# Moving q tiles, the v tile and a z tile to earlier projection stages in a hybrid layer

## The chip, the core and the metric

The kernel runs on one core of a Trainium2 chip. The metric is device time in microseconds (us) of one execution. A core has TensorE (PE; PEld is its weight load), VectorE (DVE), ScalarE (ACT), GpSimd (POOL) and SyncE (SP, which only issues DMAs here). Each works through its own queue in order, and they wait for each other by semaphores.

## The reference

One decoder layer on 1024 tokens of width 1024. One input projection feeds two mixers: a state space scan (Mamba-2, 16 heads in 2 groups, chunks of 128 tokens), and attention over the 256 best keys per query, which a small indexer scores. Their outputs are concatenated and projected, then comes a gated feed-forward network with a convolution.

```python
proj = x @ w_in                                     # 1024 x 4696
z, xbc, dt_raw, q, k, v, qi, ki, wi = split(proj)
xbc = silu(causal_dwconv(xbc, width 4))             # x: 1024, B: 256, C: 256 columns
y = ssd_scan(xs, dt, a, bm, cm) + d_skip * xs       # 8 chunks, state carried on
y_ssd = rms_norm(y * silu(z), by group) * ssd_norm_g
score = sum_h wi[h] * relu(qi[h] @ ki.T)            # causal
keep = top 256 of score per query
y_att = softmax(q @ k.T / 8 on keep) @ v
m = concat(y_ssd, y_att) @ w_out
h = layer_norm(alpha * x + m)
out = layer_norm(alpha * h + (silu(gate) * up) @ w_down)   # gate, up = dwconv(h @ w_up, width 3)
```

## The kernel before

All matmuls of the projections are made of three: weights and inputs are split into a high and a low part, and `three` (L157 to L161) adds high by high, high by low and low by high. A weight tile is loaded by SyncE (L140, L151), its high part made by GpSimd (L129) and its low part too (L132).

The input projection is cut into tiles. Tiles "c" 0 to 11 are the convolution's columns (8 and 9 are B of the two groups, 10 and 11 are C, 0 to 3 and 4 to 7 the x columns of the two groups), "q" 0 to 7 and "k" 0 and 1 the attention's columns, of 128 columns each; "z" 0 to 3 and "v" 0 are tiles of 256 columns. A c, q or k tile is two halves of 24 matmuls, 128x512 each (`proj` in PSUM). A z or v tile is eight blocks of 24 matmuls, 128x256 each (`tps`). ScalarE evicts each of them. q, k, v and z are stored to DRAM and loaded again later; a c tile stays on chip: ScalarE makes the first tap of the convolution (L481), VectorE the three others (L484), ScalarE the SiLU, and for x columns TensorE transposes it (`xsp`) into `xs`.

Beside the projections run, as generators that yield after each step:

- the scores (L303 to L309), while stage 0 of the projections runs;
- the search for the 256th best score (`topk_gen`): 32 rounds, one bit each. In a round three blocks of queries are counted on VectorE (L347) and three on ScalarE (L350), then VectorE makes the next candidate (L355, L357, L364). Behind the rounds come the masks of six blocks, L384 to L407, all on VectorE;
- the state space scan of each group (`ssd_gen`), 8 chunks: a DMA (L522), ScalarE (L526, L528), VectorE (L532, L533), GpSimd (L536 to L540), TensorE (`yoff`, `stps`, `yps`), VectorE (`off` L547, `state` L555, `xs` L563);
- the gate of each group (`gate_gen`), which loads z again (L572) and ends with transposes (`yT`) that are stored for the output projection;
- the load of k (`k_load`).

A table, `STAGES`, has the order of the projection tiles: stage 0 beside the scores, stage 1 alone, stage 2 beside the scan of group 0, stage 3 beside the gate of group 0, and stage 4 beside `k_load`, the scan of group 1 and then its gate. `par` takes a step of each in turn, and `weave` takes two steps of the search for every five of all this. The order of SyncE's queue is the order in which the code is written. On the other engines a scheduler orders the instructions when the kernel is built, by priority (the scan's is raised by 100) and by its own estimate of when each is ready; from then on the order is fixed. Behind all this come the q and v loads and the attention, whose first matmuls are `lgps` (L677).

Of the kernel before, what the change touches and what calls it, by code (L numbers as in the profile page):

```python
# [57 lines left out]
def hybrid_layer(ctx, tc, x, w_in, ssd_conv_w, ssd_conv_b, dt_bias, a_log, d_skip, ssd_norm_g,  # L58
# [18 lines left out]
    def big(name, dtype=F32, shape=(P, 1024), tag="t4"):  # L77
        return pool.tile(list(shape), dtype, name=name, tag=tag, bufs=BUFS[tag])

    def bank(name, tag, shape=(P, 512)):  # L80
        return psum.tile(list(shape), F32, name=name, tag=tag, bufs=PBUFS[tag])
# [236 lines left out]
    def topk_gen():  # L318
# [56 lines left out]
        for e, ch in enumerate(CHAINS):  # L375
            for i, (b, eng) in enumerate(ch):
# [32 lines left out]


    STAGES = ([("k", 0), ("k", 1), ("q", 0), ("q", 1), ("q", 2), ("c", 8), ("c", 10)],
# [4 lines left out]
    stream = [("c", QI0 + t * P) for t in range(1, 4)]  # L416
    for kind, i in [u for st in STAGES for u in st]:
        if kind in "ckq":
# [20 lines left out]
    for t in range(4):  # L439
        w = w_qi if t == 0 else next_w()  # L440
        a, c = big("qsa", F32R, tag="pp"), big("qsb", F32R, tag="pp")
# [594 lines left out]
    for j in range(NF):  # L1036
# [13 lines left out]
        c = bank("pc", "tp")  # L1050
# [221 lines left out]
```

## Time and profile before

| | us |
|---|---|
| median of 3 runs | 1705.73 (1703.85 to 1708.65) |
| profiled execution | 1701.0 |
| its span, first to last instruction | 1699.1 |
| PE busy | 1590.0 (94%) |
| DVE busy | 1218.1 (72%) |
| ACT busy | 917.5 (54%) |
| POOL busy | 882.0 (52%) |

A busy share is a mean over the whole span, and the stages differ. The slices of the profile show PE at nine tenths or more in most of them, and at seven to eight tenths in some between 200 and 510 us, where the search runs and DVE is at nine. Matmuls overlap, so the time of one in a row (0.39 us) is longer than the distance to the next. An "idle before" in brackets is time in which the engine had nothing to run, and the name behind the arrow is what ended it.

### The profile page before, as it was taken

Reading aid. Unit: us, or ns where it says so; the run is one execution under the profiler, and the core shown is the slowest. Engines: PE = TensorE matmul, PEld = TensorE weight load, DVE = VectorE, ACT = ScalarE, POOL = GpSimd, SP = SyncE. Lnnn points to the kernel's source line nnn. Section 1 sums busy time; section 2 is a strip of 40 time slices with the busy share of each in tenths; the row PEclk is TensorE's granted clock in tenths of the full one; section 3 lists DMA queues with packets and bytes.
Section 4 is the critical chain, followed back from the end, with each engine's and each line's share of the span. In section 5 each row is a group of like instructions: output and inputs, shape, how many; then the busy total and the mean of one; then the engine's idle time right before and its main releaser. Section 6 shows DMA issues by size and latency. Waiting matters only on the chain.

```text
span 1699.1 us, 23245 instructions
## 1 busy us (share of the span) xinstructions
PE 1590.0 (94%) x7844; PEld 1319.0 (78%) x7844; DVE 1218.1 (72%) x2274; ACT 917.5 (54%) x1759; POOL 882.0 (52%) x659
## 2 busy tenths in 40 slices
PE   8999998797989989999999993999999999999997
PEld 6888887685878867777888772878888888878886
DVE  2644689999893467777787479677777777756468
ACT  3433597687633566676676444555555555542141
POOL 2153225644257253555464356666777676475490
PEclk9999998998989999999999995999999999999999
DMA  5042032131433664554454442233444433698782
GB/s 172 16 123 63 17 103 84 43 109 57 131 91 99 179 193 110 149 151 131 147 153 151 157 162 74 87 118 131 140 138 136 132 118 118 225 351 299 237 278 109
DMA packets 208846, 232.86 MB, mean 137 GB/s; under 512 B 14051, under 2 KB 138327, under 8 KB 208727
## 3 DMA queue, kind: packets, MB, share of 16 engines
q1 hardware_dynamic: 160999, 159.79, 31.4%
q10 hardware_dynamic: 47728, 71.58, 11.6%
q8 instruction: 62, 1.02, 0.3%
q14 instruction: 57, 0.47, 0.1%
HBM read 159.70 MB, written 71.63 MB: 136 GB/s over the span
## 4 chain that ended last, share of the span: by engine, by line
PE 47%; DVE 5%; DMA 2%; ACT 1%; issue 1%; POOL 0%; SPq 0%; ACTq 0%; DVEq 0%; POOLq 0%
PE acc L159 4%; PE acc L160 4%; PE acc L161 4%; PE pa L159 2%; PE pd L159 2%; PE pa L161 2%; PE pa L160 2%; PE pc L159 2%; PE pc L160 2%; PE pd L161 2%; PE pc L161 2%; PE pd L160 2%; PE ops L160 2%; PE ops L159 2%; PE ops L161 2%; PE ptp L692 2%
## 5 line engine op out<-in xcount | busy, mean ns | idle before, releaser
L159 PE MATMUL proj<-xTh,w_hi 128*128 128x512 f32 (+1 forms) x432 | 173.0, 401 | 7.0 <-ACT xbc L478 3.5
L161 PE MATMUL proj<-xTh,w_lo 128*128 128x512 f32 (+1 forms) x432 | 170.7, 397 | 2.9 <-POOL w_lo L132 2.9
L160 PE MATMUL proj<-xTl,w_hi 128*128 128x512 f32 (+1 forms) x432 | 171.5, 397 | 0.0
L686 POOL TENSOR_SCALAR prob<-prob,sm 128x512 f32<-128x512 f32 (+7 forms) x128 | 97.1, 769 | 142.8 <-DVE sm L685 104.6
L999 POOL TENSOR_TENSOR w_hl<-s,w_hl 128x512 fp32r<-128x512 f32 x88 | 121.4, 1385 | 61.3 <-ACT w_hl L998 57.0
L129 POOL TENSOR_SCALAR w_hi<-w_raw 128x1024 fp32r<-128x1024 f32 x35 | 46.3, 1325 | 184.4 <-PE proj L160 124.4
L132 POOL TENSOR_TENSOR w_lo<-w_raw,w_hi 128x1024 fp32r<-128x1024 f32 (+1 forms) x45 | 113.1, 2516 | 27.1 <-ACT w_hi L131 24.9
L160 PE MATMUL acc<-wd_hl,g_hl 128*128 128x512 f32 x308 | 120.4, 391 | 0.0
L161 PE MATMUL acc<-wd_hl,g_hl 128*128 128x512 f32 x308 | 120.1, 391 | 0.0
L999 POOL TENSOR_TENSOR w_hl<-w_raw,w_hl 128x512 fp32r<-128x512 f32 x66 | 90.3, 1371 | 55.9 <-ACT w_hl L998 53.7
L683 ACT ACTIVATE prob<-prob,mx 128x512 f32<-128x512 f32 (+7 forms) x128 | 98.5, 771 | 36.6 <-DVE mx L680 35.9
L694 ACT ACTIVATE pt<-ptp 128x512 fp32r<-128x512 f32 x144 | 81.3, 595 | 64.7 <-PE ptp L692 43.7
L159 PE MATMUL acc<-wd_hl,g_hl 128*128 128x512 f32 x308 | 112.5, 392 | 3.3 <-ACT wd_hl L1157 3.3
L159 PE MATMUL ops<-w_hi,y_hi 128*128 128x512 f32 x256 | 102.4, 400 | 6.1 <-ACT y_hi L131 3.2
L350 ACT ACTIVATE junk<-score,cand 128x1024 bf16<-128x1024 f32 (+2 forms) x96 | 86.0, 895 | 38.5 <-DVE cand L364 35.4
L695 DVE TENSOR_TENSOR pt<-ptp,pt 128x512 fp32r<-128x512 f32 x144 | 95.6, 685 | 15.1 <-ACT pt L694 14.6
L1158 POOL TENSOR_TENSOR wd_hl<-keep,wd_hl 128x512 fp32r<-128x512 f32 x55 | 81.4, 1505 | 44.8 <-ACT wd_hl L1157 42.1
L159 PE MATMUL tps<-w_hi,xTh 128*128 128x256 f32 x320 | 95.8, 300 | 8.8 <-ACT tout L614 7.6
L159 PEld LDWEIGHTS proj<-xTh,w_hi 128*128 128x128 f32 (+1 forms) x432 | 82.2, 190 | 26.2 <-ACT xbc L478 3.9
L160 PE MATMUL ops<-w_lo,y_hi 128*128 128x512 f32 x256 | 101.5, 396 | 0.4 <-DVE w_lo L132 0.4
L161 PE MATMUL ops<-w_hi,y_lo 128*128 128x512 f32 x256 | 100.4, 395 | 0.0
L161 PEld LDWEIGHTS proj<-xTh,w_lo 128*128 128x128 f32 (+1 forms) x432 | 81.8, 189 | 21.0 <-POOL w_lo L132 4.1
(346 smaller groups left out, 5010.1 us busy)
## 6 DMA issues: line engine op xcount, KB each, us to landing
w_raw<-in_ffn_w_up_dram SPq DMA_DIRECT2D x44, 512.0 KB, 4.0
g_hl<-gs_dr SPq DMA_DIRECT2D x44, 512.0 KB, 5.5
w_raw<-in_w_in_dram SPq DMA_DIRECT2D x36, 512.0 KB, 4.9
r_dr<-rout ACTq DMA_DIRECT2D x48, 256.0 KB, 2.2
g_dr<-gt ACTq DMA_DIRECT2D x33, 256.0 KB, 2.9
keep<-in_ffn_w_down_dram SPq DMA_DIRECT2D x33, 256.0 KB, 5.7
acsb<-a_dr SPq DMA_DIRECT2D x16, 512.0 KB, 4.2
w_raw<-in_w_out_dram SPq DMA_DIRECT2D x16, 512.0 KB, 4.4
```

What stands on the lines that cost most here:

```text
L129: nc.gpsimd.tensor_scalar(hi, raw, 1.0, 1.0, op0=OP.mult, op1=OP.mult)
L132: (nc.vector if lo_on_dve else nc.gpsimd).tensor_tensor(lo, raw, f(hi), op=OP.subtract)
L159: nc.tensor.matmul(ps, ah, bh, start=start, stop=False, skip_group_check=onto)
L160: nc.tensor.matmul(ps, ah, bl, start=False, stop=False, skip_group_check=onto)
L161: nc.tensor.matmul(ps, al, bh, start=False, stop=stop, skip_group_check=onto)
L350: nc.scalar.activation(junk[1][:, :n], score_ap[b], AF.Sign, bias=c, scale=-1.0, accum_out=val[e][:, i:i + 1])
L683: nc.scalar.activation(t[:, :w], t[:, :w], AF.Exp, bias=mx[:, h:h + 1], scale=-1.0, accum_out=sm[:, h:h + 1])
L686: nc.gpsimd.tensor_scalar(t[:, :w], t[:, :w], sm[:, 4 + h:5 + h], 1.0, op0=OP.mult, op1=OP.mult)
L694: nc.scalar.activation(pt[:, 0], ps, AF.Copy)
L695: nc.vector.tensor_tensor(pt[:, 1], ps, f(pt[:, 0]), op=OP.subtract)
L999: nc.gpsimd.tensor_tensor(t[:, 1], src, f(t[:, 0]), op=OP.subtract)
L1158: nc.gpsimd.tensor_tensor(wt[:, 1], w_raw, f(wt[:, 0]), op=OP.subtract)
```

## The change

Only the table differs. Tiles q 3 and q 4 move from stage 2 to stage 1, between the c tiles; q 5 and v 0 move from stage 4 to stage 2; z 2 moves from stage 4 to stage 3, between c 4 and c 5. Stage 4 keeps z 3, q 6 and q 7.

```diff
     STAGES = ([("k", 0), ("k", 1), ("q", 0), ("q", 1), ("q", 2), ("c", 8), ("c", 10)],
-              [("c", 0), ("c", 1), ("c", 2), ("c", 3)],
-              [("z", 0), ("z", 1), ("q", 3), ("q", 4)],
-              [("c", 9), ("c", 11), ("c", 4), ("c", 5), ("c", 6), ("c", 7)],
-              [("z", 2), ("z", 3), ("v", 0), ("q", 5), ("q", 6), ("q", 7)])
+              [("c", 0), ("q", 3), ("c", 1), ("c", 2), ("q", 4), ("c", 3)],
+              [("z", 0), ("z", 1), ("q", 5), ("v", 0)],
+              [("c", 9), ("c", 11), ("c", 4), ("z", 2), ("c", 5), ("c", 6), ("c", 7)],
+              [("z", 3), ("q", 6), ("q", 7)])
```

VectorE's queue before, at the end of the search and the start of the masks. `cand` is the search's candidate, `conv_3559` is c 5, `conv_3670` is c 6, and L384 is the first operation of the masks:

```order
L364 SCALAR_TENSOR_TENSOR cand0_4340<-fail0_4338,cand0_4324 128x2
L484 SCALAR_TENSOR_TENSOR conv_3559<-xbc_3560,cw_656,conv_3559 128x1023
L357 TENSOR_TENSOR fail1_4346<-val1_1579,thr1_1578 128x4
L484 SCALAR_TENSOR_TENSOR conv_3559<-xbc_3560,cw_656,conv_3559 128x1022
L364 SCALAR_TENSOR_TENSOR cand1_4348<-fail1_4346,cand1_4334 128x4
L484 SCALAR_TENSOR_TENSOR conv_3559<-xbc_3560,cw_656,conv_3559 128x1021
L484 SCALAR_TENSOR_TENSOR conv_3670<-xbc_3671,cw_656,conv_3670 128x1023
L484 SCALAR_TENSOR_TENSOR conv_3670<-xbc_3671,cw_656,conv_3670 128x1022
L484 SCALAR_TENSOR_TENSOR conv_3670<-xbc_3671,cw_656,conv_3670 128x1021
L384 TENSOR_SCALAR eq_4510,cnt_4511<-score_693,cand0_4340 128x1024
```

The same place after the change; `conv_3731` is c 4, `conv_4197` is c 5, `conv_4312` is c 6. Ahead of these rows, behind the last candidate, stand the taps of c 9, the eight L585 of group 0's gate and the taps of c 11:

```order
L484 SCALAR_TENSOR_TENSOR conv_3731<-xbc_3732,cw_656,conv_3731 128x1023
L484 SCALAR_TENSOR_TENSOR conv_3731<-xbc_3732,cw_656,conv_3731 128x1022
L484 SCALAR_TENSOR_TENSOR conv_3731<-xbc_3732,cw_656,conv_3731 128x1021
L484 SCALAR_TENSOR_TENSOR conv_4197<-xbc_4198,cw_656,conv_4197 128x1023
L484 SCALAR_TENSOR_TENSOR conv_4197<-xbc_4198,cw_656,conv_4197 128x1022
L484 SCALAR_TENSOR_TENSOR conv_4197<-xbc_4198,cw_656,conv_4197 128x1021
L484 SCALAR_TENSOR_TENSOR conv_4312<-xbc_4313,cw_656,conv_4312 128x1023
L484 SCALAR_TENSOR_TENSOR conv_4312<-xbc_4313,cw_656,conv_4312 128x1022
L384 TENSOR_SCALAR eq_4784,cnt_4785<-score_693,cand0_4614 128x1024
L387 TENSOR_SCALAR pen_4787<-score_693,cand0_4614 128x1024
L484 SCALAR_TENSOR_TENSOR conv_4312<-xbc_4313,cw_656,conv_4312 128x1021
```

The masks stand behind c 6 in both; the taps of the other c tiles have moved from between the rounds to behind them, while z 2 has moved to between c 4 and c 5 in TensorE's queue.

TensorE's queue before, at the seventh chunk of group 1 (`yoff`, `stps` and `yps` belong to the scan, `tps` to the v tile):

```order
L160 MATMUL tps_4908<-w_lo_4748,xTh_113 128x256
L545 MATMUL yoff_5054<-state_4867,conv_3272 128x512
L161 MATMUL tps_4908<-w_hi_4747,xTl_121 128x256
L159 MATMUL tps_4908<-w_hi_4747,xTh_113 128x256
L160 MATMUL tps_4908<-w_lo_4748,xTh_113 128x256
L161 MATMUL tps_4908<-w_hi_4747,xTl_121 128x256
L159 MATMUL tps_4991<-w_hi_4555,xTh_114 128x256
```

The fifth to the seventh chunk of group 1 after the change, from the last projection on (`ops` is the output projection):

```order
L161 MATMUL proj_5106<-xTh_117,w_lo_4933 128x512
L545 MATMUL yoff_5183<-state_5093,conv_3606 128x512
L551 MATMUL stps_5188<-xdd_5178,btok_5158 128x512
L561 MATMUL yps_5193<-xdt_5177,lmat_5162 128x64 x8
L545 MATMUL yoff_5243<-state_5190,conv_3606 128x512
L551 MATMUL stps_5248<-xdd_5231,btok_5158 128x512
L561 MATMUL yps_5253<-xdt_5230,lmat_5215 128x64 x8
L545 MATMUL yoff_5300<-state_5250,conv_3606 128x512
L551 MATMUL stps_5305<-xdd_5288,btok_5158 128x512
L561 MATMUL yps_5310<-xdt_5287,lmat_5272 128x64 x8
```

The last four chunks have no projection between them any more; one chunk more and then `ops` and `yT` follow.

## Rows read from the trace of the kernel before

**Rows 1.** The page's head.

```profile
span 1699.1 us, 23245 instructions
```

**Rows 2.** Windows: length; busy PE, PEld, DVE, ACT, POOL; clock; DMA share, GB/s.

```profile
353.00:429.00 76.00, 66.44 (x279) 52.80 (x278) 69.59 (x153) 60.73 (x122) 31.63 (x19) 0.91 0.27 82
429.00:505.00 76.00, 66.79 (x453) 60.39 (x452) 74.30 (x106) 39.35 (x89) 29.30 (x19) 0.93 0.40 117
505.00:556.00 51.00, 48.55 (x350) 43.72 (x350) 22.69 (x28) 17.82 (x42) 36.22 (x28) 0.97 0.35 98
556.00:600.00 44.00, 44.00 (x219) 37.12 (x219) 18.43 (x21) 23.73 (x45) 14.14 (x7) 1.00 0.67 193
```

**Rows 3.** Timeline of VectorE, end of the search: start, length, instruction, idle before.

```profile
423.77 0.16 DVE L364 SCALAR_TENSOR_TENSOR cand<-fail,cand 128x4 int32<-128x4 int32 x1
423.89 1.28 DVE L484 SCALAR_TENSOR_TENSOR conv<-xbc,cw,conv 128x1021 f32<-128x1021 f32 x1
429.96 5.16 DVE L484 SCALAR_TENSOR_TENSOR conv<-xbc,cw,conv 128x1023 f32<-128x1023 f32 x3 [4.79 <-ACT conv L481]
435.04 1.27 DVE L384 TENSOR_SCALAR_CACHE_REDUCE eq<-score,cand 128x1024 bf16<-128x1024 f32 x1
```

**Rows 4.** Timeline of ScalarE, the eviction of c 6.

```profile
428.05 0.60 ACT L478 ACTIVATE xbc<-proj 128x512 f32<-128x512 f32 x1 [0.69 <-PE proj L161]
```

**Rows 5.** Timeline of VectorE, from the last mask to the last chunk.

```profile
503.87 1.57 DVE L407 SCALAR_TENSOR_TENSOR mask<-score,cand,eq 128x512 bf16<-128x512 f32 x1
...
533.15 0.69 DVE L547 TENSOR_TENSOR off<-yoff,dtset 128x512 f32<-128x512 f32 x1 [3.42 <-PE stps L551]
537.58 0.69 DVE L563 TENSOR_TENSOR xs<-yps,skip 128x512 f32<-128x512 f32 x1 [3.73 <-POOL skip L548]
...
545.63 0.69 DVE L547 TENSOR_TENSOR off<-yoff,dtset 128x512 f32<-128x512 f32 x1 [6.37 <-PE stps L551]
...
551.87 0.69 DVE L547 TENSOR_TENSOR off<-yoff,dtset 128x512 f32<-128x512 f32 x1 [3.17 <-PE yoff L545]
...
554.96 0.69 DVE L563 TENSOR_TENSOR xs<-yps,skip 128x512 f32<-128x512 f32 x1 [0.43 <-PE yps L561]
```

**Rows 6.** Timeline of TensorE, the attention's first matmul.

```profile
600.15 0.36 PE L677 MATMUL lgps<-kh,qst 128*128 128x256 f32 x1
```

**Rows 7.** Timeline of VectorE, rounds of the search with little between them.

```profile
353.40 1.13 DVE L347 TENSOR_SCALAR_CACHE_REDUCE junk<-score,cand 128x896 bf16<-128x896 f32 x1
...
361.51 1.15 DVE L347 TENSOR_SCALAR_CACHE_REDUCE junk<-score,cand 128x896 bf16<-128x896 f32 x1
```

**Rows 8.** Timeline of TensorE, the eighth chunk of group 0.

```profile
349.51 1.89 PE L561 MATMUL yps<-xdt,lmat 128*128 128x64 f32 x16
```

**Rows 9.** Timeline of TensorE: matmuls six apart (proj) and nine apart (tps).

```profile
456.83 0.28 PE L160 MATMUL tps<-w_lo,xTh 128*128 128x256 f32 x1
...
457.91 0.28 PE L160 MATMUL tps<-w_lo,xTh 128*128 128x256 f32 x1
...
592.76 0.39 PE L161 MATMUL proj<-xTh,w_lo 128*128 128x512 f32 x1
...
594.12 0.39 PE L161 MATMUL proj<-xTh,w_lo 128*128 128x512 f32 x1
```

**Rows 10.** Timeline of TensorE, its waits between 385 and 397 us.

```profile
389.39 0.50 PE L159 MATMUL proj<-xTh,w_hi 128*128 128x512 f32 x1 [1.87 <-POOL w_hi L129]
...
393.60 0.79 PE L159 MATMUL proj<-xTh,w_hi 128*128 128x512 f32 x1 [3.47 <-ACT xbc L478]
...
396.78 0.79 PE L161 MATMUL proj<-xTh,w_lo 128*128 128x512 f32 x1 [1.97 <-POOL w_lo L132]
```

**Rows 11.** Timeline of GpSimd, ahead of the wait at 537 us.

```profile
533.92 2.37 POOL L132 TENSOR_TENSOR w_lo<-w_raw,w_hi 128x1024 fp32r<-128x1024 f32 x1
```

**Rows 12.** Timeline of TensorE, the first chunk of group 1.

```profile
474.74 3.68 PE L561 MATMUL yps<-xdt,lmat 128*128 128x64 f32 x16 [2.49 <-DVE lmat L533]
```

## The prediction

> **What bounds the kernel now.** The profiled execution took 1701.0 us for a span of 1699.1 us [rows 1]. The runs have a median of 1705.73 us, 4.7 us above it. The sum below is made in the profiled execution, and its difference is added to the median.
>
> I first read the table by stretches. Between 353 and 600 us, where the change acts, TensorE is not the bound everywhere [rows 2]. Up to 505 us VectorE is busy for 69.59 of 76 and then 74.30 of 76 us, while TensorE has gaps and a granted clock of 0.91 and 0.93. From 505 us it turns round: VectorE works 22.69 of 51 us, and from 556 to 600 us TensorE is busy for all 44.00 us, with projections that nothing else waits for. So the stretch up to 505 us is paced by VectorE's queue, and the one behind it is filled by TensorE.
>
> Next, VectorE's own timeline at the seam [rows 3]. The bit search (L347 to L364) ends with its last `cand` at 423.77 us. From then on the masks of the attention could be made, beginning with L384. But L384 runs only at 435.04 us: ahead of it in VectorE's queue stand the taps (L484) of conv tiles 5 and 6, and tile 6's first tap waited 4.79 us for ScalarE's copy of the projection. This is the mechanism of my forecast, already there in small: the masks wait for TensorE's projection of conv tile 6. Its last matmul is done when ScalarE picks it up at 428.05 us [rows 4], 7.0 us ahead of L384.
>
> Then the way to the attention [rows 5, 6]: the last mask ends at 505.44 us, the last chunk of state space group 1 (its `xs`) starts at 554.96 us, and the first logits of the attention run at 600.15 us. The attention cannot start without the masks, and its q loads stand in SyncE's queue behind the gate of group 1.
>
> **The change part by part.** No instruction is added or removed; every tile still has its weight load on SyncE, its split on GpSimd and its stores on ScalarE's queue. What counts is where they stand. The order shows 5 steps.
>
> 1. The eighth chunk of group 0 comes later. TensorE's queue has more projections ahead of the first chunk, so VectorE goes further with the search before it: ahead of the eighth chunk's `xs` it has 76 passes of L347 where it had 63, and 9 conv taps where it had 6. Three passes make a round, and two rounds took 361.51 - 353.40 = 8.11 us where little else ran [rows 7]. So 13/3 x 4.06 = 17.6 us, and three taps of 1.28 us [rows 3] give 3.8 us, less 1 us as the search starts a little earlier: +20.4 us. The yps matmuls of that chunk ended at 349.51 + 1.89 = 351.4 us [rows 8] and now at 371.8 us. VectorE is nearly full here, so it cannot hide this; if it does, the term is 0.
>
> 2. From there to conv tile 6, TensorE has more to do. Before: 253 proj matmuls and 24 transposes. After: 236 proj, 323 tps (v and z tile 2) and 40 transposes. A proj takes (594.12 - 592.76)/6 = 0.227 us, a tps (457.91 - 456.83)/9 = 0.12 us [rows 9], and I count a transpose as a tps. That is 60.3 us before and 97.2 us after. Before, 351.4 to 428.05 is 76.7 us, so 16.4 us were lost, 7.3 us of them in three waits for weights and for an eviction that stood in ScalarE's queue among the search [rows 10]. After, only 20 of the search's 96 passes are left here (27 us of about 100), so I take 5 us lost; bounds 0 and 16.4. Tile 6 is projected at 371.8 + 97.2 + 5 = 474.0 us, 46 us later than before. The idle TensorE time that the moved work fills is real, but it lies where VectorE is waited for, and the fill stands ahead of what VectorE waits for next.
>
> 3. VectorE runs dry. The end of its search moves earlier (it has fewer taps of tiles 9, 11, 4 and 5 between its rounds), and then come the taps of tiles 11, 4, 5 and 6, with the masks behind them as before. What is queued behind the waiting tap is the whole mask block, and for that waits the attention. L384 moves from 435.04 to about 481 us. The block up to the last mask took 505.44 - 435.04 = 70.4 us and gets one more tap, so the last mask ends at 481 + 70.4 + 1.3 = 552.7 us, 47.3 us later.
>
> 4. The tail gets shorter. From the last mask to the first logits it took 600.15 - 505.44 = 94.7 us. Six chunks are left in it, before and after. Now the last four stand in TensorE's queue without projections between them, so VectorE's three long waits for TensorE (3.42, 6.37, 3.17 us) go, and so does the wait of 3.73 us for GpSimd [rows 5], which was splitting weights of a moved tile at 533.92 us [rows 11]: -16.7 us. Bounds: 0, if another link of the chunk chain is late next (GpSimd's five passes per chunk would be), and -28.3 us, all of VectorE's idle time in 505 to 556 [rows 2]. The gate, its loads of z and then of q keep their 45.2 us behind the last `xs`. First logits at 552.7 + 78.0 = 630.7 us, +30.6 us.
>
> 5. Behind the first logits the order is the same but for 8 transposes, about 1 us less. TensorE's projections no longer cover the tail: of its work between tile 6 and the first logits about 75 us are left of 132, and 474 + 75 = 549 us is well before 630, so TensorE is no bound there.
>
> Sum: +20.4 + 25.5 (97.2 + 5 - 76.7) + 1.3 - 16.7 - 1 = +29.5 us, rounded to +30: 1731 us for the profiled execution, 1736 us for the median. With the bounds of steps 2 and 4 alone it lies between +13 and +58.
>
> **The clock.** After a wait of 2.49 us the yps of one chunk took 3.68 us at a granted clock of one half, against 1.89 us [rows 8, 12], so 1.8 us more. In the tail after the change TensorE will wait before nearly every chunk. The Trainium skill (TensorE: Matmul & The Clock Gate, HAM oscillation) says that a kernel whose short bursts of matmuls are separated by waits falls back to the slow clock at each burst. By that rule the four bare chunks cost 4 x 1.8 = 7 us more, and the sum is +37; by the rows, where the chunks with full TensorE ran at 1.89 us, it is +30. I leave it in the upper part of the range.
>
> **Rivals.**
>
> A, faster: the eighth chunk is not late. If ScalarE's passes pace the search and VectorE does the additional rounds in time it now spends blocked, step 1 is 0. Tile 6 is then there at 454 us, 38 us of TensorE work later the first chunk of group 1 runs (492 us), and eight chunks at (49.5 - 13)/6 = 6.1 us and the gate's 45.2 us give 586 us, if the masks fit between the chunks: about -15 us, 1691 us. It decides once the masks no longer stand in front. For it: the chunk chain needs no mask. Against it: both are in one VectorE queue, whose order puts the last mask ahead of the third chunk, and VectorE was full.
>
> B, hardly a difference: step 1 as forecast, but the masks fit between the chunks. 474 + 38 + 49 + 45 = 606 us, +5 us, 1711 us. For it: VectorE has waits in the chunk chain to fill. Against it as in A.
>
> C, slower than forecast: 16 us lost in step 2 (z tile 2's weights are loaded behind the gate's z loads on SyncE), no gain in the tail, and the slow clock: 30 + 11 + 17 + 7 = +65 us, 1771 us; with one or two of the three, +40 to +55. For it: losses of this kind are in the trace. Against it: the waits of VectorE for TensorE lose their cause.
>
> **How the numbers follow.** Forecast 57% (its own range 1719 to 1746), A 12%, B 13%, C 18%. What a measurement can tell here is about 0.3%, 5 us. Faster by more than that: A, 12%. Within it: most of B, 9%. Slower: the rest, 79%. The range leaves a tenth on each side: below, the larger part of A (under 1700), above, the upper half of C (over 1757).
>
> **What would show it.** Right: the last `cand` well before 424 us, then L484 waiting for ScalarE's L481 for some 40 us in all before L384 near 481 us; the last mask near 553 us; in the last chunks TensorE waiting for VectorE and not the other way; first logits near 630 us. Wrong: L384 before 450 us, or the first logits before 600 us. If L384 is late and the logits are not, the mask block was not what the attention waited for, and step 3 fails. If the eighth chunk's `xs` is near 353 us, step 1 fails.

## The result, and the profile after

| | before | after |
|---|---|---|
| median | 1704.79 us (4 runs, 1703.65 to 1708.65) | 1725.47 us (4 runs, 1724.94 to 1728.46) |
| ratio, 95% interval | | 1.0123 [1.0111, 1.0136] |
| span of the profiled execution | 1699.1 us | 1723.4 us |
| first logits of the attention | 600.15 us | 625.54 us |
| from there to the end | 1098.9 us | 1097.8 us |

The change made the kernel slower by 20.7 us; 1736 were forecast, in a range of 1700 to 1757. The profiled executions differ by 24.3 us, all of it ahead of the first logits (+25.4 us there, -1.1 us behind them).

The head of the page answers to [rows 1]:

```profile
span 1723.4 us, 23264 instructions
```

The windows of the changed kernel answer to [rows 2], with one window more:

```profile
353.00:429.00 76.00, 68.85 (x381) 59.66 (x381) 67.98 (x162) 58.18 (x121) 33.98 (x22) 0.93 0.31 98
429.00:505.00 76.00, 75.93 (x506) 69.83 (x505) 29.19 (x34) 35.52 (x72) 23.47 (x12) 1.00 0.30 96
505.00:556.00 51.00, 44.12 (x248) 36.96 (x246) 50.65 (x82) 20.06 (x44) 19.84 (x14) 0.93 0.27 76
556.00:600.00 44.00, 26.63 (x116) 17.02 (x114) 22.37 (x28) 15.62 (x33) 31.11 (x25) 0.80 0.26 77
600.00:640.00 40.00, 19.71 (x80) 14.21 (x80) 23.56 (x52) 24.97 (x49) 9.51 (x8) 0.70 0.75 216
```

Between 429 and 505 us the two engines have changed places. TensorE is busy for 75.93 of 76 us where it was for 66.79, and VectorE for 29.19 where it was for 74.30. VectorE's work has slid into the next window (50.65 us for 22.69), and TensorE's idle time has gone to the end.

The seam on VectorE, which answers to [rows 3], in two pieces of its timeline (start, length, instruction, idle before):

```profile
408.63 0.16 DVE L364 SCALAR_TENSOR_TENSOR cand<-fail,cand 128x4 int32<-128x4 int32 x1
408.97 4.84 DVE L484 SCALAR_TENSOR_TENSOR conv<-xbc,cw,conv 128x1023 f32<-128x1023 f32 x3 [0.18 <-ACT conv L481]
...
432.39 4.74 DVE L484 SCALAR_TENSOR_TENSOR conv<-xbc,cw,conv 128x1023 f32<-128x1023 f32 x3 [5.43 <-ACT conv L481]
476.52 4.58 DVE L484 SCALAR_TENSOR_TENSOR conv<-xbc,cw,conv 128x1023 f32<-128x1023 f32 x3 [39.40 <-ACT conv L481]
484.70 2.60 DVE L484 SCALAR_TENSOR_TENSOR conv<-xbc,cw,conv 128x1023 f32<-128x1023 f32 x2 [3.60 <-ACT conv L481]
487.22 1.27 DVE L384 TENSOR_SCALAR_CACHE_REDUCE eq<-score,cand 128x1024 bf16<-128x1024 f32 x1
```

The search ends 15.1 us earlier than before, and the masks (L384) begin 52.2 us later. In one wait VectorE stands still for 39.40 us: its first tap of c 5 waits for ScalarE's tap (L481), that one for ScalarE's copies of the projection (L478), and those for TensorE, which works on z 2 first. ScalarE's timeline shows it (it answers to [rows 4]); of the copies, the first is the second half of c 4, the next two are c 5, the last two c 6:

```profile
430.05 0.60 ACT L478 ACTIVATE xbc<-proj 128x512 f32<-128x512 f32 x1 [2.00 <-PE proj L161]
...
462.01 0.60 ACT L478 ACTIVATE xbc<-proj 128x512 f32<-128x512 f32 x1 [5.08 <-PE proj L161]
...
469.14 2.44 ACT L526 ACTIVATE lmat<-acsb,dtset 128x128 f32<-128x128 f32 x8
471.48 0.58 ACT L478 ACTIVATE xbc<-proj 128x512 f32<-128x512 f32 x1
...
475.25 1.24 ACT L481 ACTIVATE conv<-xbc,cw 128x1024 f32<-128x1024 f32 x1
476.38 0.59 ACT L478 ACTIVATE xbc<-proj 128x512 f32<-128x512 f32 x1
...
478.33 0.60 ACT L478 ACTIVATE xbc<-proj 128x512 f32<-128x512 f32 x1 [0.42 <-PE proj L161]
```

Not all of the wait is TensorE's. By count, the last of the 24 matmuls for the second half of c 5 ended at 467.4 us, but ScalarE copied that half at 471.48 and made the tap at 475.25 us, since the scan's `lmat` (L526, L528) stands ahead of both in its queue: some 7 of the 39.40 us. Little of this reaches the masks, which wait for c 6: from the end of its copy to L384 it took 8.3 us, and 6.4 us before.

The tail on VectorE answers to [rows 5]. VectorE still waits for TensorE, though no projection stands between the chunks:

```profile
555.57 1.76 DVE L407 SCALAR_TENSOR_TENSOR mask<-score,cand,eq 128x512 bf16<-128x512 f32 x1
...
569.65 0.69 DVE L547 TENSOR_TENSOR off<-yoff,dtset 128x512 f32<-128x512 f32 x1 [2.50 <-PE stps L551]
...
578.19 0.69 DVE L547 TENSOR_TENSOR off<-yoff,dtset 128x512 f32<-128x512 f32 x1 [1.51 <-PE stps L551]
...
585.92 0.69 DVE L547 TENSOR_TENSOR off<-yoff,dtset 128x512 f32<-128x512 f32 x1 [3.55 <-PE stps L551]
...
593.74 0.69 DVE L575 TENSOR_TENSOR xs<-xs,zs 128x512 f32<-128x512 f32 x1 [4.10 <-ACT zs L573]
594.35 0.68 DVE L563 TENSOR_TENSOR xs<-yps,skip 128x512 f32<-128x512 f32 x1
```

And TensorE there, up to the first logits [rows 6]. It waits for VectorE's `state`, then for the whole gate:

```profile
559.01 1.12 PE L545 MATMUL yoff<-state,conv 128*128 128x512 f32 x2 [0.23 <-DVE state L555]
561.28 1.12 PE L551 MATMUL stps<-xdd,btok 128*128 128x512 f32 x2 [0.22 <-POOL xdd L538]
562.24 1.89 PE L561 MATMUL yps<-xdt,lmat 128*128 128x64 f32 x16
...
574.37 2.07 PE L545 MATMUL yoff<-state,conv 128*128 128x512 f32 x2 [3.03 <-DVE state L555]
576.24 1.91 PE L551 MATMUL stps<-xdd,btok 128*128 128x512 f32 x2
577.94 2.58 PE L561 MATMUL yps<-xdt,lmat 128*128 128x64 f32 x16
...
613.82 0.80 PE L159 MATMUL ops<-w_hi,y_hi 128*128 128x512 f32 x1 [22.52 <-ACT y_hi L131]
...
625.54 0.36 PE L677 MATMUL lgps<-kh,qst 128*128 128x256 f32 x1
```

### The profile page after: what moved, and what is told of

Read it like the earlier page. It is cut to its first block, busy times and chain, and to the rows that moved or that the text cites. A ratio compares the mean times of both kernels' runs of the same rounds, so it can differ in the third digit from the quotient of the medians.

```text
span 1723.4 us, 23264 instructions
## 1 busy us (share of the span) xinstructions
PE 1590.0 (92%) x7844; PEld 1315.7 (76%) x7844; DVE 1213.3 (70%) x2274; ACT 920.1 (53%) x1761; POOL 883.7 (51%) x659
## 3 DMA queue, kind: packets, MB, share of 16 engines
q10 hardware_dynamic: 47728, 71.58, 11.5%
## 4 chain that ended last, share of the span: by engine, by line
PE 66%; DVE 19%; ACT 6%; issue 4%; DMA 4%; POOL 2%; SPq 0%; ACTq 0%; DVEq 0%; POOLq 0%
PE acc L160 4%; PE acc L159 4%; PE acc L161 4%; PE proj L161 3%; PE proj L159 3%; PE proj L160 3%; DVE junk L347 3%; PE ops L161 3%; PE ptp L692 3%; PE ops L160 3%; PE ops L159 3%; PE pa L159 2%; PE pd L159 2%; PE pd L161 2%; PE pc L160 2%
## 5 line engine op out<-in xcount | busy, mean ns | idle before, releaser
L159 PEld LDWEIGHTS proj<-xTh,w_hi 128*128 128x128 f32 (+1 forms) x432 | 81.2, 188 | 20.4 <-issue 2.8
L309 DVE SCALAR_TENSOR_TENSOR score<-relu,wq,score 128x1024 f32<-128x1024 f32 (+5 forms) x42 | 50.5, 1203 | 64.4 <-ACT relu L305 63.8
```

The costliest lines, as they stand in the source:

```text
L159: nc.tensor.matmul(ps, ah, bh, start=start, stop=False, skip_group_check=onto)
```

## The experiments

Twelve kernels were run. The first theory was that of the prediction; from e5 on it is that the masks and the scan of group 1 both wait for the late c tiles. The table has the marks of all: the end of ScalarE's copy of c 6 (L478), the first mask operation (L384), the end of the last one (L407), the start of the last chunk's `xs`, the end of the last projection on TensorE and the first logits, in us of the profiled executions.

| kernel | c 6 | L384 | last mask | last xs | last proj. | logits | median | ratio |
|---|---|---|---|---|---|---|---|---|
| before | 428.6 | 435.0 | 505.4 | 555.0 | 595 | 600.1 | 1704.79 | 1 |
| e4 before, masks early | 439.8 | 422.5 | 488.6 | 558.0 | 598 | 603.3 | 1707.39 | 1.0017 [1.0001, 1.0033] |
| e9 q 3, q 4 late | 421.5 | 426.7 | 492.4 | 547.1 | 610 | 607.8 | 1714.21 | 1.0063 [1.0039, 1.0087] |
| e6 q 5, v 0 early | 450.9 | 457.3 | 525.1 | 575.0 | 576 | 607.8 | 1708.98 | 1.0028 [1.0014, 1.0042] |
| e5 q 3, q 4 early | 440.1 | 446.5 | 510.8 | 567.9 | 604 | 610.0 | 1718.36 | 1.0080 [1.0063, 1.0098] |
| e2 z 2 back | 454.1 | 460.5 | 527.3 | 577.2 | 578 | 610.1 | 1712.74 | 1.0046 [1.0028, 1.0064] |
| e7 z 2 back, masks early | 470.1 | 411.8 | 488.9 | 574.2 | 582 | 610.3 | 1712.44 | 1.0061 [1.0040, 1.0081] |
| e1 masks early | 483.0 | 412.2 | 479.5 | 577.8 | 564 | 613.0 | 1716.60 | 1.0062 [1.0045, 1.0080] |
| e8 z 2 cut to 2 of 8 | 467.9 | 476.4 | 544.0 | 585.5 | 553 | 616.9 | 1726.51 | 1.0131 [1.0116, 1.0146] |
| e10 z 2 behind c 7 | 456.2 | 462.6 | 531.8 | 586.4 | 577 | 617.5 | 1717.66 | 1.0089 [1.0068, 1.0110] |
| e12 z 2 cut to 4 of 8 | 470.1 | 478.5 | 546.2 | 588.5 | 555 | 620.6 | 1723.87 | 1.0120 [1.0102, 1.0137] |
| e3 z 2 alone | 456.5 | 467.3 | 540.9 | 585.0 | 599 | 623.2 | 1726.19 | 1.0117 [1.0098, 1.0136] |
| after | 478.9 | 487.2 | 557.3 | 594.3 | 566 | 625.5 | 1725.47 | 1.0123 [1.0111, 1.0136] |
| e11 z 3 cut to 2 of 8 | 476.9 | 484.9 | 551.8 | 592.6 | 535 | 626.5 | 1736.05 | 1.0191 [1.0170, 1.0212] |

Ratios are to the kernel before on the same chip (1704.45 beside e1 to e4, 1703.61 beside e5 to e8, 1703.92 beside e9 to e12).

**e1, masks early** (edit of the changed kernel)

```diff
-TK = 2
+TK = 3
```

> The changed kernel, same table of stages, but the search gets three steps where it had two (TK 3), so that the masks are written into the program ahead of conv tiles 5 to 7: in VectorE's queue L384 then stands 2 taps behind the last candidate, not 14. TensorE's order stays nearly the same, and so does the eighth chunk (step 1). Theory M (the masks, queued behind the taps of tiles 5 and 6, delay the attention): L384 near 415 us, VectorE's wait of 39 us is filled with masks, the chunks of group 1 run without them at about 6 us each behind the first one (near 522 us), first logits near 600 us, -25 us against the changed kernel: about 1700 us, 0.986 of it, and no slower than before. Rival U (the tail without projections is what costs, wherever the masks stand): the same uncovered tail, so within 5 us of the changed kernel, 1725 us.

8.9 us of the 20.7 came back, about a third of the 25 us that theory M expected; the logits came 12.5 us earlier. The masks now run from 412.2 to 479.5 us, before c 6 is there. VectorE's timeline of this kernel shows what is late in their place:

```profile
496.08 5.17 DVE L484 SCALAR_TENSOR_TENSOR conv<-xbc,cw,conv 128x1023 f32<-128x1023 f32 x3 [3.48 <-ACT conv L481]
508.06 0.29 DVE L532 TENSOR_TENSOR cbm<-cbps,tri 128x128 f32<-128x128 f32 x1 [6.81 <-PE cbps L530]
```

The taps are those of c 7, the second row is the scan of group 1. So the masks are one of two things that wait for the late projections; the scan is the other.

**e2, z 2 back** (edit of the changed kernel)

```diff
-              [("c", 9), ("c", 11), ("c", 4), ("z", 2), ("c", 5), ("c", 6), ("c", 7)],
-              [("z", 3), ("q", 6), ("q", 7)])
+              [("c", 9), ("c", 11), ("c", 4), ("c", 5), ("c", 6), ("c", 7)],
+              [("z", 2), ("z", 3), ("q", 6), ("q", 7)])
```

> The changed kernel with z tile 2 alone put back into the last stage: 192 tps matmuls x 0.12 = 23 us of TensorE work leave the place ahead of conv tile 5. Theory M: L384 goes from 487 to about 464 us, the last mask to 534 us, first logits to about 605 us, about -20 us: 1705 us, about the time before. Rival S (the late eighth chunk, that is the q tiles ahead of the scan, is what costs): it stays late, so little changes, 1720 us or more.

12.7 us came back, of some 20 forecast. c 6 comes 24.9 us earlier (192 `tps` of 0.12 us are 23.0 us), L384 26.8 and the last mask 30.0 us. The logits gain less, 15.5 us.

**e3, z 2 alone** (edit of the kernel before: the same move, nothing else)

```diff
-              [("c", 9), ("c", 11), ("c", 4), ("c", 5), ("c", 6), ("c", 7)],
-              [("z", 2), ("z", 3), ("v", 0), ("q", 5), ("q", 6), ("q", 7)])
+              [("c", 9), ("c", 11), ("c", 4), ("z", 2), ("c", 5), ("c", 6), ("c", 7)],
+              [("z", 3), ("v", 0), ("q", 5), ("q", 6), ("q", 7)])
```

> The kernel before with z tile 2 alone moved to between conv tiles 4 and 5; q tiles and v stay where they were, so the eighth chunk is not late and the tail keeps v and three q tiles as cover. Theory M: tile 6 is projected up to 23 us later (some of it is hidden in TensorE's waits), L384 at 450 to 458 us instead of 435, the last mask at 520 to 528 us, first logits 8 to 18 us later: 1713 to 1723 us. Rival U (the tail): it is still covered, no change, 1705 us. Rival S (the eighth chunk): no change, 1705 us.

This one move costs 21.7 us, as much as the whole change, and more than was forecast: L384 comes 32.3 us later (15 to 23 forecast) and the logits 23.1 us later (8 to 18). The eighth chunk of group 0 is not late here (its `xs` at 353.7 us), and projections last until 599 us. VectorE's timeline at its seam:

```profile
454.52 6.65 DVE L484 SCALAR_TENSOR_TENSOR conv<-xbc,cw,conv 128x1023 f32<-128x1023 f32 x3 [31.37 <-ACT conv L481]
464.77 2.60 DVE L484 SCALAR_TENSOR_TENSOR conv<-xbc,cw,conv 128x1023 f32<-128x1023 f32 x2 [3.60 <-ACT conv L481]
467.29 1.27 DVE L384 TENSOR_SCALAR_CACHE_REDUCE eq<-score,cand 128x1024 bf16<-128x1024 f32 x1
```

It is the wait of the changed kernel, 31.37 us of it. So this wait needs neither the late eighth chunk nor the bare tail.

**e4, the kernel before with TK = 3** (the edit of e1)

> The kernel before with TK 3, the control to the first run: what earlier masks do where nothing delays them. Theory M: VectorE gains only its wait of 5 us and TensorE, full from 556 us on, still sets the first logits at 600 us: within 5 us of before, 1700 to 1710 us. If TK 3 by itself were what is worth 25 us, this kernel would be near 1680 us.

The last mask ends 16.8 us earlier and no time is gained: in the kernel before, the masks alone are not what the end waits for.

**e5, q 3 and q 4 alone** (edit of the kernel before)

```diff
-              [("c", 0), ("c", 1), ("c", 2), ("c", 3)],
-              [("z", 0), ("z", 1), ("q", 3), ("q", 4)],
+              [("c", 0), ("q", 3), ("c", 1), ("c", 2), ("q", 4), ("c", 3)],
+              [("z", 0), ("z", 1)],
```

> The kernel before with q 3 and q 4 in stage 1 alone; stage 2 is then z 0 and z 1, and nothing else moves. Theory (what counts is when TensorE projects c 4 to c 7, because the masks of the attention and the scan of group 1 both wait for them): the eighth chunk of group 0 comes about 13 us later (near 366 us), but TensorE has two tiles less between it and c 6, so c 6 and c 7 come at about the time of before (c 7 at 440 to 452 us), the first logits at 598 to 608 us, the median at 1702 to 1711. Rival (the late eighth chunk is itself the cost, carried through to the end): +10 to +13 us, 1715 to 1718, first logits near 612 us.

My theory missed, and the rival came near: logits at 610.0 us, and 14.8 us lost where it had 10 to 13. The eighth chunk is 10.5 us late, for about 13 expected, but c 6 is not on time (440.1 us), though TensorE has two tiles less ahead of it. TensorE's timeline says why:

```profile
376.41 0.80 PE L159 MATMUL proj<-xTh,w_hi 128*128 128x512 f32 x1 [4.08 <-POOL w_hi L129]
...
384.14 0.80 PE L161 MATMUL proj<-xTh,w_lo 128*128 128x512 f32 x1 [5.01 <-POOL w_lo L132]
...
402.95 0.80 PE L159 MATMUL proj<-xTh,w_hi 128*128 128x512 f32 x1 [6.04 <-POOL w_hi L129]
```

and GpSimd's timeline what stood ahead of those splits:

```profile
396.17 1.28 POOL L575 TENSOR_TENSOR xs<-xs,zs 128x512 f32<-128x512 f32 x1 [3.25 <-ACT zs L573]
400.62 1.27 POOL L575 TENSOR_TENSOR xs<-xs,zs 128x512 f32<-128x512 f32 x1 [3.17 <-ACT zs L573]
401.85 2.05 POOL L129 TENSOR_SCALAR w_hi<-w_raw 128x1024 fp32r<-128x1024 f32 x2
```

The weights of the c tiles wait in GpSimd's queue behind the gate of group 0, and those rows wait for ScalarE. This queue I had not counted. So the late eighth chunk does cost time, by way of the gate behind it.

**e6, q 5 and v 0 alone** (edit of the kernel before)

```diff
-              [("z", 0), ("z", 1), ("q", 3), ("q", 4)],
+              [("z", 0), ("z", 1), ("q", 3), ("q", 4), ("q", 5), ("v", 0)],
...
-              [("z", 2), ("z", 3), ("v", 0), ("q", 5), ("q", 6), ("q", 7)])
+              [("z", 2), ("z", 3), ("q", 6), ("q", 7)])
```

> The kernel before with q 5 and v 0 in stage 2 alone, behind q 4; q 3 and q 4 stay where they were. Theory (late c tiles): the eighth chunk of group 0 stays near 353 us, but about 35 us of projections more stand on TensorE ahead of c 6, some of which fill gaps: c 7 at 465 to 480 us, L384 at 460 to 472 us, first logits at 615 to 627 us, the median at 1720 to 1732. Rival (the late eighth chunk is the cost): no change, 1702 to 1710. Rival (only a z tile between c 4 and c 5 hurts, since it parts the c tiles from each other): less than 8 us, under 1713.

My theory held only in its first half: the eighth chunk on time (352.8 us), c 6 22.2 us later, the last mask 19.7 and the last `xs` 20.0 us later. But the logits came only 7.6 us later, since the gate took 32.8 us (575.0 to 607.8) where it took 45.2. The second rival, that only a z tile between c 4 and c 5 hurts, had less than 8 us and under 1713, and that came: 5.4 us and 1708.98. Its reason does not stand: e5 moves no z tile and costs 14.8 us, and here c 6 is late without one.

**e7, z 2 back and masks early** (the edits of e1 and e2 together)

> The changed kernel with z 2 back in stage 4 and with TK = 3 (the search and its masks are taken 3 steps for 5 of the rest, so the masks stand ahead of the late taps on VectorE). Theory (two waits side by side, masks and scan, both behind c 7's projection; each of the two edits alone gave back 9 to 13 us of 21): the masks are out of the way near 480 us, c 7 comes at 465 to 480 us, and the scan of group 1 sets the end: its last chunk at 565 to 575 us, first logits at 602 to 608 us, the median at 1703 to 1711. If the two edits just added up (9 + 13 of 21): 1704. If they buy the same thing, as where the masks alone had mattered: 1712 to 1716.

As much as e2 alone. Its last mask ends 38.4 us earlier than in e2, its c 6 comes 16.0 us later, and the last `xs` is the same within 3 us.

**e8 and e12, z 2 shorter** (edits of the changed kernel; the diff is that of e12, with four of eight steps, e8 has two)

```diff
-            for k in range(NK):
+            for k in ((0, 1, 4, 5) if d0 == 512 else range(NK)):
...
```

The rest of the edit, not shown, marks the last step of the shorter sum. What is left out is part of the layer's computation.

> The changed kernel, with the sums of z tile 2 cut to 2 of their 8 steps (this part of the computation is left out): z 2 stays between c 4 and c 5 but takes 8 blocks of 6 matmuls for 24, 144 matmuls of 0.12 us or 17 us less of TensorE, and nothing is put into the last stage for it. Theory (late c tiles): c 7 comes 15 to 18 us earlier (474 to 477 us), L384 near 470 us, first logits at 607 to 613 us, the median at 1708 to 1715, about as with z 2 put back. Rival (the tail lacks the cover of projections, which putting z 2 back gave it): the tail is as bare as with the change, so under 5 us come back, 1720 to 1727.

> The changed kernel, with the sums of z tile 2 (between c 4 and c 5) cut to 4 of their 8 steps; this part of the computation is left out. 8 blocks of 12 matmuls, 96 x 0.12 = 11.5 us less of TensorE ahead of c 5. Cutting them to 2 of 8 (17 us less) brought c 6 11 us and the first logits 8.6 us earlier, and yet no time, since the stretch behind the first logits was 10 us longer there. Theory (late c tiles): c 6 at 470 to 474 us, first logits at 618 to 621 us; the stretch behind them 1098 to 1100 us as with the change, so 1718 to 1722. If the longer stretch behind belongs to such a cut: 1725 to 1730.

Up to the logits they follow the dose: 11.5 us less of TensorE brought c 6 8.8 us and the logits 4.9 us earlier, 17 us less 11.0 and 8.6 us. For e8 the theory had forecast 12 to 18 us for the logits. The medians didn't follow. The stretch behind the logits took 1101.9 and 1108.3 us where it took 1097.8, and 1723.87 and 1726.51 us are no gain on 1725.47; e8's median lies where its rival (the bare tail) had it, at 1720 to 1727, though the logits moved by more than that rival allows. The projections, masks and scan explain the first part; the second stays open.

**e9, q 3 and q 4 the other way** (edit of the kernel before)

```diff
-              [("z", 0), ("z", 1), ("q", 3), ("q", 4)],
+              [("z", 0), ("z", 1)],
...
-              [("z", 2), ("z", 3), ("v", 0), ("q", 5), ("q", 6), ("q", 7)])
+              [("z", 2), ("z", 3), ("v", 0), ("q", 3), ("q", 4), ("q", 5), ("q", 6), ("q", 7)])
```

> The kernel before with q 3 and q 4 moved the other way, from stage 2 to stage 4, between v 0 and q 5. Theory (VectorE's path: search, taps of c 5 and c 6, masks, scan of group 1; it is full between 353 and 505 us in the kernel before, so projecting c 5 to c 7 earlier than before gains little, while the gate at the end gets 22 us of TensorE work more to carry): last mask 495 to 508 us, first logits 600 to 615 us, the median 1704 to 1718. Rival (each move to an earlier place costs, so the opposite one gains): first logits 580 to 592 us, 1685 to 1697.

As my theory had it, apart from a last mask 2.6 us earlier than its bound. The last `xs` comes 7.9 us earlier, but projections go on until 610 us, and the attention starts no earlier than 607.8. Too little can stand at the end, and too much.

**e10, z 2 behind c 7** (edit of the changed kernel)

```diff
-              [("c", 9), ("c", 11), ("c", 4), ("z", 2), ("c", 5), ("c", 6), ("c", 7)],
+              [("c", 9), ("c", 11), ("c", 4), ("c", 5), ("c", 6), ("c", 7), ("z", 2)],
```

> The changed kernel with z 2 behind c 7 in the same stage instead of between c 4 and c 5. Theory (what counts is what TensorE has ahead of c 5 to c 7): about the time of the kernel with z 2 back in the last stage, 1709 to 1716, c 6 near 454 us, first logits 607 to 613 us. Rival (what counts is that z 2 leaves the last stage, where it covered the wait of the gate): 1720 to 1727, first logits 619 to 626 us.

Between the two forecasts: 1717.66 us. c 6 and the masks come as in e2 (within 5 us), and 7.8 us came back. The last `xs` is 9.2 us later than in e2, where the same z 2 stands in the last stage, and so are the logits, by 7.5 us. How late the c tiles are is therefore not all of z 2's price: about half of the 15.5 us that e2 gave the logits goes with its place behind them. What holds the scan up there is not shown.

**e11, z 3 shorter** (edit of the changed kernel: as e8, with z 3 for z 2)

> The changed kernel, with the sums of z tile 3 (in the last stage, behind c 7) cut to 2 of their 8 steps; this part of the computation is left out. That is 144 matmuls of 0.12 us, 17 us less of TensorE, the same amount as in the run with z tile 2 cut, but behind c 7. Theory (VectorE's path): TensorE has idle time in this place anyway, so c 7 within 3 us of 492, first logits 620 to 627 us, the median 1718 to 1727. Rival (the sum of TensorE's work up to the first logits decides): 17 us come back, first logits near 608 us, 1707 to 1711.

The logits came at 626.5 us, 0.9 us later than with the change: TensorE's work behind c 7 was no bound. That the median is 10.6 us higher neither theory has. Its profiled execution (1732.3 us) is the fastest of its four, and 6.2 of the 7.1 us by which its span is longer lie behind the logits.

**What the runs say together.** In the eleven kernels with the masks behind c 6 (TK = 2), L384 starts 5.2 to 10.8 us behind the end of the copy of c 6, and the last mask ends 64.2 to 73.6 us behind L384, although c 6 itself moves by 57 us (421.5 to 478.9). This link is nearly rigid. The next is elastic, 37.0 to 57.1 us from the last mask to the last `xs`. The last is a floor or a cover: where the projections end before 583 us, the logits come 31 to 36 us behind the last `xs`; where they end at 595 us or later and the last `xs` by 568 us, they come within 7 us of the end of the projections. e3, with both of them late, takes 38.2 us.

## Why the prediction was right

| step | forecast | measured |
|---|---|---|
| 1: end of the eighth chunk's yps, from 351.4 us | +20.4 | +23.1 (374.5) |
| 2: from there to c 6 | 102.2 us | 103.8 us (478.33) |
| 3: L384 | about 481 us | 487.22 us |
| 3: from L384 to the end of the last mask | 71.7 us | 70.1 us |
| 4: from the last mask to the last xs | -16.7 | -12.5 (37.0 for 49.5) |
| 4: from the last xs to the logits | 0 | -14.0 (31.2 for 45.2) |
| 5: behind the logits | -1 | -1.1 |

Measured, the steps add up to 52.2 (L384) - 0.3 - 12.5 - 14.0 - 1.1 = +24.3 us for the profiled executions, for which +30 was forecast; the medians differ by 20.7. That the total came so near is in part luck: without the last term of step 4 the sum is 8.8 us above the forecast, and that term is 14.0 us below it.

**Steps 1 to 3 held.** The eighth chunk was late (by 2.7 us more than forecast; the search, from which step 1 had taken 1 us for an earlier start, started 0.3 us later), VectorE did not hide it, and z 2 and v lengthened TensorE's way to c 6 by what their matmuls take. The 5 us put down as lost on that way are borne out: TensorE's waits between 374 and 478 us add up to 3.2 us, the longest 2.15 us, and behind it matmuls of a projection ran 0.43 us apart instead of 0.227 for a while. VectorE then waited 5.43 + 39.40 + 3.60 us for L481, where "some 40 us in all" were forecast. L384 is 6 us later than forecast, by the sum of steps 1 and 2 (4.3 us) and by 1.9 us behind the copy of c 6. That rivals A and B fail is in the same rows: the eighth chunk's `xs` stood at 376.3 us, and the masks did not fit between the chunks, since they began only at 487 us and VectorE was then full, 50.65 of 51 us up to 556 us. Of rival C's losses, 16 us on the way to c 6 and a tail that gains nothing, neither came; its slow clock came in part.

**The mis-sized term is in step 4: "The gate, its loads of z and then of q keep their 45.2 us behind the last `xs`."** They took 31.2 us. From the gate's first block (L573) to its eighth it was 25.4 us before and 14.1 after; that is 11.3 of the 14.0 us. ScalarE's timeline of the kernel before shows three blocks and, among them, a copy of a projection tile (`tout` is v), which waits for TensorE:

```profile
556.90 0.63 ACT L573 ACTIVATE zs<-zs 128x512 f32<-128x512 f32 x1 [0.73 <-DMA zs<-z_dr]
558.05 0.39 ACT L614 ACTIVATE tout<-tps 128x256 f32<-128x256 f32 x1 [0.52 <-PE tps L161]
...
561.22 0.62 ACT L573 ACTIVATE zs<-zs 128x512 f32<-128x512 f32 x1
...
564.29 0.62 ACT L573 ACTIVATE zs<-zs 128x512 f32<-128x512 f32 x1
```

and after the change nothing but the gate:

```profile
595.15 0.61 ACT L573 ACTIVATE zs<-zs 128x512 f32<-128x512 f32 x1
...
597.21 0.63 ACT L573 ACTIVATE zs<-zs 128x512 f32<-128x512 f32 x1
```

A block takes 2.0 to 2.1 us where it took 2.0 to 4.9. Two things go with the long ones. Copies stand in ScalarE's queue between the blocks and wait there for TensorE. And between the second and the third of the blocks shown, where VectorE's part (L575) took 1.75 us for 0.69, GpSimd split weights at the same time. From the kernel before, with the split of q that the logits wait for (L655):

```profile
560.68 2.39 POOL L132 TENSOR_TENSOR w_lo<-w_raw,w_hi 128x1024 fp32r<-128x1024 f32 x1
561.87 1.75 DVE L575 TENSOR_TENSOR xs<-xs,zs 128x512 f32<-128x512 f32 x1 [3.61 <-ACT zs L573]
...
594.37 2.39 POOL L655 TENSOR_TENSOR qst<-qraw,qst 64x1024 fp32r<-64x1024 f32 x1 [2.84 <-ACT qst L654]
```

and the same split after the change:

```profile
622.76 2.40 POOL L655 TENSOR_TENSOR qst<-qraw,qst 64x1024 fp32r<-64x1024 f32 x1 [6.46 <-ACT qst L654]
```

I had called the projections of that stretch something "that nothing else waits for". The gate's copies waited for them, and at the end the logits did: q was ready at 596.76 us, and the logits stood 3.4 us longer behind the projections and the first output projections on TensorE. After the change it is 0.4 us, so 3.0 of the 14.0 us lie there. e6 shows this term alone: the last `xs` 20.0 us later, the gate 12.4 us shorter, the logits +7.6.

**Step 4's other half was too large.** VectorE's waits for TensorE did not go with the projections. They shrank to 2.50, 1.51 and 3.55 us, because in the bare tail each engine waits for the other: TensorE 3.03 and 1.90 us for `state`, VectorE for `stps` after it. That is the "other link late next" of the bounds, and GpSimd, which they name, is part of it: it is busy for 31.11 of the 44 us, and in the chain of work that ended last its passes (L548, L554, L536, L538) take 13.0 of the 19.0 us from 554.7 to 573.6. The border to the gate is not sharp either: the last `xs` stood behind the gate's first L575, which waited 4.10 us for z. The inputs of that `xs` were there some 3 us earlier, so some 3 us could be counted to the other half.

**"What is queued behind the waiting tap is the whole mask block, and for that waits the attention" was half of the mechanism.** By it, e1 should have given back nearly all of the 25.4 us that the first logits had lost; it gave 12.5. The scan of group 1 waits for c 7 as well. e4, e7 and e1 say the same: where the masks stand decides little alone. How late c 4 to c 7 are projected bears on both, but e10, with the c tiles of e2 and logits 7.5 us later, shows that it does not decide all. What I can't derive is how the parts add up: e3, e5 and e6 alone cost 21.7, 14.8 and 5.4 us, 41.9 together, and the change with all of them 20.7. Two reasons are visible. The gate can be shortened only once, down to some 31 us, and in e3, where projections lasted until 599 us, it was shortened by 7 us alone. And the waits for GpSimd in e5 are not in the changed kernel, where z and v tiles stand in their place.

**The clock.** In the bare tail the granted clock was 0.80 (556 to 600 us) and 0.70 (600 to 640), means between the two levels of 1.2 and 2.4 GHz. Up to 565.8 us projections stand beside the chunks, and the chunks at 559 and 566 us ran at a granted clock of 1.00 (559 to 571 us). Behind the wait of 3.03 us, yoff took 2.07, stps 1.91 and yps 2.58 us, where the chunk at 559 us took 1.12, 1.12 and 1.89. With the chunk after it, the rows add up to 4.1 us more of matmul time; the price by the rule was 7 us, and I had left it out of the sum. The rule of the Trainium skill (TensorE: Matmul & The Clock Gate, HAM oscillation), that short bursts between waits fall back to the slow clock, is borne out by the chunks at 574 and 582 us, behind waits of 3.03 and 1.90 us (granted clock 0.59 and 0.67). The last chunk's yoff came without a wait and took 1.12 us again, so two of the four bare chunks paid.

**What stays open** is the stretch behind the first logits. Its work is the same in all kernels, bar a few transposes and first matmuls of the output projection, and it took 1097.8 to 1108.7 us. In e8, e11 and e12, which do less on TensorE ahead of it, it was 4 to 10 us longer than with the change; but in e4, e5 and e9, which leave nothing out, it was 7 to 11 us longer, so that the shorter sums are its cause is not shown. Each kernel has one profiled execution, and e9's was the slowest of its four. No run tells why, so a difference of 5 us between two medians of the table proves no step; the marks ahead of the logits do.

## What to carry to other kernels

Idle time of TensorE is not free room. Ask what the waiting engine waits for next on TensorE: a tile that only a much later stage reads belongs behind it, and z 2 ahead of c 5 cost as much as the whole change, though TensorE had 9 us of idle time in that window. Price the stretch that work is taken from as well: filler at the end also holds up the evictions and the queue of what it covers, and here its leaving gave back 14.0 us. And moving the block that is seen to wait (the masks) buys only the time to the next one that waits for the same tiles.

## What had not been expected of the hardware

VectorE's L575 of group 1 is eight operations of 128x512 in each of the fourteen kernels. The 96 of them with no GpSimd operation beside them took 0.69 us each; of the 16 with one, the longest, beside weight splits, took 2.63 to 2.94 us. So a GpSimd pass that VectorE does not wait for goes with a longer step of VectorE's chain.

Less TensorE work made no faster kernel: e11 left out 144 matmuls of 0.12 us and took 1736.05 us, against 1725.47 with them; why is open. And within one kernel and order, runs lay up to 10 us apart (1703.83 to 1714.13 us in e4), as much as several of the effects studied here.
